# v of 14 heads turned by transposing transfers instead of TensorE transposes

## The chip, the cores and the metric

One core of a Trainium2 chip runs one launch of the kernel. The metric is the device time of that launch in microseconds, the median of several runs. The engines named below: PE is TensorE (matmuls, and PEld its weight loads), DVE is VectorE, ACT is ScalarE, POOL is GpSimd, SP is SyncE, which here only issues transfers.

## The reference, cut to what matters

One layer, 512 tokens (S) of width 2048 (D), 16 heads of 128: eight with stick-breaking attention (A), eight with banded chunk attention (B).

```python
h = rms_norm(x, norm_g[layer])
proj = jnp.einsum('bsd,de->bse', h, w_in[layer])
qa, ka, va, ga, qb, kb, vb, gb = jnp.split(proj, splits, axis=-1)
ya = stick_breaking_attention(split_heads(qa, N_HEADS_SB), ...)
yb = chunk_band_attention(split_heads(qb, N_HEADS_CH), ...)
mixed = jnp.concatenate([merge_heads(ya) * jax.nn.silu(ga),
                         merge_heads(yb) * jax.nn.silu(gb)], axis=-1)
x = x + jnp.einsum('bse,ed->bsd', mixed, w_out[layer])
```

In both kinds of attention the last step for a head is a product of weights (tokens by tokens) with v (tokens by 128). For that product v has to have its tokens on the partitions.

## The kernel before, in words

**Units and stages.** The input projection is computed transposed, with features on the partitions and tokens along the row. It is cut into 32 units of 256 columns. Four units make a group of two heads: unit 4g gives q, 4g+1 k, 4g+2 v and 4g+3 the gate; the head's number is n = 2g + h. Each product is done as a Winograd-like scheme with seven products instead of eight, and in two pieces of precision: every operand is split into a rounded high part and a low rest (ACT casts, DVE subtracts), and the matmuls of high by high, low by high and high by low are added up. 28 of the 32 units are "major" (`MAJOR`: units 3 to 30): such a unit runs seven stages, each of eight pairs of matmuls, one of 512 and one of 256 columns (lines 849 and 851). The weights of a stage are loaded by SP (line 520, and 536 for one block), summed by DVE (548) or by adding transfers from POOL (540, 559), and split by ACT (579) and DVE (580) into one of three buffers, which PE's stage releases when it is done.

**Joining a unit.** `chain(m)` brings a major unit's seven products together. Its working tile `c` has four spaces in the arena. It claims three of them when the unit's first product is there and the fourth after the second product; ACT copies products into `c` (607, 612, 615, 628), DVE adds and subtracts others (617 and the same helper line), and at the end one DVE sum of 1024 elements (632) adds the two halves of `c` and writes the unit's tile `t`, which is `C[g, kind]`, 128 features by two heads by 512 tokens. Then the four spaces are released and ("unit", u) is marked done.

**v of a head.** `v_turn` waits for the unit 4g+2, and for ("values", n-1), since there is one buffer for v. It takes one of three spare PSUM banks, issues four TensorE transposes of 128 by 128 (line 1529), and ACT copies the four blocks back into `C[g, 2]` while it scales each row by `rstd` (line 1534). Then ACT casts the high part of v (1537) and DVE writes the rest (1538) into the tile `v`. `values` multiplies the turned attention weights `wth` and `wtl` with it on PE. For the last heads the result is multiplied by the gate (1569) and stored by SP (1575). Attention weights are turned by PE too (1506); the first turn of head n waits for the values of head n-1.

**Order.** No engine chooses at run time. A list scheduler in the Python code plays the whole run through with its own cost per operation (`Op(engine, cost, fn, due, lag)`; `AC`, `DV` and `M` make such entries for ACT, DVE and PE) and writes each engine's instructions in the order in which it plays them, by due time. For a transfer it adds `lag` bytes at 290e3 bytes per microsecond and a landing of 2.4 us. On the chip each engine works through its list in order and waits at semaphores. SP's list is one queue for all loads and stores.

**The tail.** Units 28 to 31 are put in the order 28, 29, 27, 30, 31. After unit 31 the output projection runs over the stored heads; some of its operands (`xbwth`, `xbwtl`, written by ACT at line 763) lie in the buffers of the turned attention weights, and may be written only after the values of head 15.

Of the kernel before, what the change touches and what calls it, by code (L numbers as in the profile page):

```python
# [7 lines left out]

F32 = mybir.dt.float32
F32R = mybir.dt.float32r  # L10
BF16 = mybir.dt.bfloat16
AF = mybir.ActivationFunctionType
ALU = mybir.AluOpType
PSUM = bass.MemoryType.PSUM

P = 128
S = 512
D = 2048
NT = S // P
# [11 lines left out]
H = 256  # L31
# [46 lines left out]
def trunk_kernel(ctx: ExitStack, tc: tile.TileContext, xT, xn, wi, wqk, wo, ng, qg, kg, rel, out):  # L78
# [29 lines left out]
    act, dve, pe, sp, pool = nc.scalar, nc.vector, nc.tensor, nc.sync, nc.gpsimd  # L108

    def single(shape, name, dt=F32):  # L110
        return cp.tile(shape, dt, tag=name, name=name)

    def tmp(shape, tag, name, dt=F32, bufs=1):
        return wp.tile(shape, dt, tag=tag, name=name, bufs=bufs)
# [7 lines left out]
    rstd = single([P, NT], "rstd")  # L122
# [4 lines left out]
    R = single([P, S], "R")  # L127
# [17 lines left out]
    def avail(r):  # L145

        return all(r[1] <= x[0] or x[1] <= r[0] for x in taken.values())

    def claim(key, r):
        assert avail(r), (key, r, taken)  # L150
        taken[key] = r
        return arena[:, r[0]:r[1]] if r[0] < 100 * KB else parts[:, r[0] - 100 * KB:r[1] - 100 * KB]

    def unclaim(key):
        del taken[key]
# [7 lines left out]
    clock = [0.0]  # L163
# [5 lines left out]
    done = set()  # L169
# [19 lines left out]
    def DV(w, fn, due=None, n=1):  # L189
        return Op("DVE", (0.075 + 1.04e-3 * w) * n, fn, due)  # L190

    def AC(w, fn, due=None, n=1):
        return Op("ACT", (0.085 + 0.85e-3 * w) * n, fn, due)
# [4 lines left out]
    def M(cost, fn):  # L198
        return Op("PE", cost, fn, 0.0)
# [85 lines left out]
    def major(u):  # L285
        return u in MAJOR
# [87 lines left out]
    def need(k, before=0.0):  # L374

        return lambda: clock[0] + begins[k] - begins[position[0]] - before
# [119 lines left out]
    def stage(m, p):  # L496
        return step_of[MAJOR[m], p]
# [87 lines left out]
    def major_bank(u, p):  # L585
        return (3 * MAJOR.index(u) + 3 + BANK_OF[p]) % 5

    def chain(m):
        u = MAJOR[m]
        b = [banks[:, major_bank(u, p), :] for p in (0, 1, 5)]  # L590
        k = [at_step[stage(m, p)] for p in range(NP)]
        there = lambda p: lambda: ("stage", m, p) in done

        def free(p):
            x = major_bank(u, p)
            del holder[2 * x], holder[2 * x + 1]

        yield there(0)
        def space(i):
            w = (CMB[1] - CMB[0]) // 4  # L600
            return CMB[0] + i * w, CMB[0] + (i + 1) * w

        c = arena[:, CMB[0]:CMB[1]].rearrange("p (a b) -> p a b", a=4)
        for i in (0, 1, 2):
            yield lambda: avail(space(i))
            claim(("cmb", m, i), space(i))
        yield AC(512, lambda: act.copy(c[:, 0, :], b[0]), need(k[2], AHEAD[5]))
        done.add(("before", m, 2))
        yield there(1)
        yield lambda: avail(space(3))  # L610
        claim(("cmb", m, 3), space(3))
        yield AC(512, lambda: act.copy(c[:, 3, :], b[1]), need(k[3], AHEAD[5]))
        done.add(("before", m, 3))
        yield there(2)
        yield AC(512, lambda: act.copy(c[:, 2, :], b[0]), need(k[4], AHEAD[5]))
        done.add(("before", m, 4))
        join = lambda i, x, y, op=ALU.subtract: lambda: dve.tensor_tensor(out=c[:, i, :], in0=x, in1=y, op=op)  # L617
        yield there(3)
        yield DV(512, join(2, b[1], c[:, 2, :]), clock[0] + 3)
        free(1)  # L620
        yield there(4)
        yield DV(512, join(3, c[:, 3, :], b[0]), need(k[6], AHEAD[6]))
        done.add(("before", m, 6))
        yield there(5)
        yield DV(512, join(0, b[2], c[:, 0, :], ALU.add), clock[0] + 3)
        free(5)
        yield there(6)
        yield AC(512, lambda: act.copy(c[:, 1, :], b[0]), clock[0] + 1)
        free(0)
        _, t = yield from result(u, 0)  # L630
        t_ = t.rearrange("p a (b c) -> p (a b) c", c=H)
        yield DV(1024, lambda: dve.tensor_tensor(out=t_, in0=c[:, :, :H], in1=c[:, :, H:], op=ALU.add), clock[0] + 1.5)  # L632
        for i in range(4):
            unclaim(("cmb", m, i))
        done.add(("unit", u))
# [153 lines left out]
    def place(u, a, half):  # L789
        b = unit_banks(u, a)  # L790
        half = ALONE[u >= NU][half] if alone(u) else ENDS[half] if u == NU + 3 and a else half
        return b[half // 2] * 2 + half % 2
# [3 lines left out]
    for k in reversed(range(len(program))):  # L796
        n, x, a = program[k]
        u = steps_[n][0]
        b = major_bank(*steps_[n]) if major(u) else place(u, a, x[2]) // 2
# [121 lines left out]
    def result(u, a):  # L921

        if u >= NU:
            tag = (("wth", "wtl"), ("cv", "cg"))[u % 2][a]
            yield lambda: ("co", tag) not in done and all(("released", j, 1) in done for j in range(NJ) if HOME[j] == tag)
            done.add(("co", tag))
            t = tmp([P, 2, S], tag, f"co{u}_{a}")

            return [t.rearrange("p h (b f c) -> p h b f c", f=2, c=P)[:, :, :, f, :] for f in range(2)], t
        tag = ("cq", "ck", "cv", "cg")[u % 4]  # L930
        yield lambda: emptied(tag, u // 4 - 1)
        C[u // 4, u % 4] = t = tmp([P, 2, S], tag, f"c{u}")
        v = t.rearrange("p a (b c) -> p a b c", c=H)
        return [v[:, 0], v[:, 1]], t
# [257 lines left out]
    def emptied(tag, g):  # L1192

        n = head(g, 1)
        k = ("cq", "ck", "cv", "cg").index(tag)
        if g < 0:

            return ("released", k + 2, 0) in done
        if k == 0 and g % 2 and ("read", n, 2) not in done:
            return False  # L1200
        return (("read", n, 0), ("read", n, 1), ("c_v", g), ("store", g, 1))[k] in done
# [74 lines left out]
    C = {}  # L1276
    qk, vv, wt, wT, tm, bias = {}, {}, {}, {}, {}, {}
# [3 lines left out]
    def take(who):  # L1281

        yield lambda: len(owner) < len(SPARE)
        i = next(i for i in SPARE if i not in owner)
        owner[i] = who
        return i

    def give(i):
        del owner[i]
# [18 lines left out]
    def head(g, h):  # L1308
        return 2 * g + h
# [185 lines left out]
    def turn(n, b, src, k):  # L1495
# [20 lines left out]
        give(i)  # L1516
        done.add(("turned", n, b))

    def v_turn(g, h):
        n = head(g, h)  # L1520
        yield lambda: "R" in done and ("unit", 4 * g + 2) in done
        yield lambda: ("values", n - 1) in done if n else all(("staged", j, 0) in done for j in range(NJ))
        i = yield from take(("v", g, h))
        f = C[g, 2][:, h, :]
        b = banks[:, i, :]

        def fn():
            for t in range(NT):
                pe.transpose(b[:, t * P:(t + 1) * P], f[:, t * P:(t + 1) * P], ident)  # L1529

        yield M(0.5, fn)

        for t in range(NT):
            yield Op("ACT", 0.31, lambda: act.activation(f[:, t * P:(t + 1) * P], b[:, t * P:(t + 1) * P], AF.Copy, scale=rstd[:, t:t + 1]))
        give(i)
        d = vv[n] = tmp([P, 2, S], "v", "v", F32R)
        yield AC(512, lambda: act.copy(d[:, 0, :], f))
        yield DV(512, lambda: dve.tensor_tensor(out=d[:, 1, :], in0=f, in1=d[:, 0, :].bitcast(F32), op=ALU.subtract))
        done.add(("v read", n))
        done.add(("v", g, h))  # L1540
# [84 lines left out]
    for m in range(NM):  # L1625
        for x in ("A11", "A21", "A22", "A12"):
            spawn(block_load(m, x), (0, stage(m, 0)))
        spawn(block_s1(m), (0, stage(m, 0)))
        spawn(block_sums(m), (0, stage(m, 0)))
        for p in range(NP):  # L1630
            spawn(block_split(m, p), (0, stage(m, p)))
        spawn(chain(m), (0, 0))
# [3 lines left out]
    for g in range(NG):  # L1636
        for h in range(2):
            n = head(g, h)
            if g % 2:
                spawn(prep_q(g, h), (n, 0, 0))  # L1640
            for kind in range(2):
                spawn((prep_b if g % 2 else prep_a)(g, kind, h), (n, 0, kind))
            if g % 2:
                spawn(load_bias(g, h), (n, 0))
            spawn(score(g, h), (n, 1))
            spawn(v_turn(g, h), (n, 3))
            spawn(values(g, h), (n, 4))
        spawn(gates(g), (2 * g, 5))
# [42 lines left out]
```

## Time and profile before

| | |
|---|---|
| median of 3 runs | 904.73 us (904.24 to 905.43) |
| profiled execution | 904.54 us |
| its span | 902.8 us |
| TensorE transposes of v (line 1529) | 64, in 16 groups of four |
| their copies back (line 1534) | 64, 22.0 us of ACT |

The span is the time between the first and the last instruction that the profiler recorded; the device time has 1.7 us more around it. A group of instructions is shown with its line, engine, shapes and count, then busy time and mean duration in ns, then the idle time before it and what ended that. Matmuls are pipelined, so the durations of neighbours overlap: what one costs the stream is read from start to start.

### The profile page before, as it was taken

The page shows a single profiled execution, that of the slowest core. Times are in us where ns is not written, and L with a number is a line of the kernel's source. Part 1 is how long each engine was busy: PE and PEld are TensorE (multiplying, and loading weights), DVE is VectorE, ACT ScalarE, POOL GpSimd, SP SyncE. Part 2 cuts the span into 40 slices and gives each one's busy share as a digit, 9 for nine tenths or more (in the row PEclk, how much of TensorE's full clock was granted, in tenths as well). Part 3 has the DMA queues.
Part 4 walks back from the last instruction along what each step waited for, and adds up shares of the span by engine and source line. Part 5 has one row for each costly group of instructions (what it writes and reads, how often), then busy time and mean ns, then how long its engine had stood idle before and what let it go on. Part 6 is the DMA issues. An engine that isn't in the chain of part 4 may idle for free.

```text
span 902.8 us, 15448 instructions
## 1 busy us (share of the span) xinstructions
PE 896.8 (99%) x5504; PEld 801.3 (89%) x5504; DVE 767.1 (85%) x1251; ACT 637.5 (71%) x1203; POOL 69.9 (8%) x96
## 2 busy tenths in 40 slices
PE   9999999999999999999999999999999999999998
PEld 7898888888888888888888888888888988999997
DVE  7999989788898878788979787889878988988785
ACT  7876968797689658885876588868767885544342
POOL 0001000000000010000000000010000000101012
PEclk9999999999999999999999999999999999999999
DMA  9777787767676887587758765776664536656371
GB/s 310 250 211 169 156 182 183 178 153 184 160 177 142 199 193 171 139 176 198 167 136 215 184 167 136 188 191 158 152 168 126 185 115 208 158 196 181 125 187 47
DMA packets 187837, 156.22 MB, mean 173 GB/s; under 512 B 9072, under 2 KB 157552, under 8 KB 187760
## 3 DMA queue, kind: packets, MB, share of 16 engines
q1 hardware_dynamic: 177680, 122.58, 44.7%
q0 software_dynamic: 9792, 32.51, 22.3%
q8 instruction: 43, 0.70, 0.3%
q14 instruction: 34, 0.28, 0.1%
q10 hardware_dynamic: 288, 0.14, 0.1%
HBM read 117.45 MB, written 8.39 MB: 139 GB/s over the span
## 4 chain that ended last, share of the span: by engine, by line
PE 98%; ACT 1%; DVE 0%; issue 0%; DVEq 0%
PE banks L849 40%; PE banks L778 21%; PE banks L851 20%; PE banks L776 10%; PE banks L1506 2%; PE banks L839 2%; PE banks L1412 1%; PE banks L840 1%; PE banks L1529 1%; PE banks L1600 0%; ACT parts L579 0%; PE banks L1338 0%; DVE co L1054 0%; ACT W L1482 0%; PE banks L1339 0%
## 5 line engine op out<-in xcount | busy, mean ns | idle before, releaser
L849 PE MATMUL banks<-x,parts 128*128 128x512 f32 x1568 | 501.2, 401 | 0.0
L851 PEld LDWEIGHTS banks<-x,parts 128*128 128x128 f32 x1568 | 294.3, 188 | 70.0 <-DVE parts L580 0.7
L851 PE MATMUL banks<-x,parts 128*128 128x256 f32 x1568 | 309.8, 279 | 0.0
L580 DVE TENSOR_TENSOR parts<-arena,parts 128x1024 fp32r<-128x1024 f32 x196 | 239.0, 1221 | 67.1 <-ACT parts L579 66.7
L579 ACT CAST parts<-arena 128x1024 fp32r<-128x1024 f32 x196 | 205.9, 1051 | 111.2 <-PE banks L849 81.5
L849 PEld LDWEIGHTS banks<-x,parts 128*128 128x128 f32 x1568 | 240.5, 189 | 0.8
L778 PE MATMUL banks<-parts,x 128*128 128x256 f32 (+1 forms) x672 | 134.5, 298 | 0.0
L458 ACT CAST parts<-arena 128x1024 fp32r<-128x1024 f32 (+2 forms) x86 | 76.8, 908 | 68.0 <-PE banks L778 31.0
L778 PEld LDWEIGHTS banks<-parts,x 128*128 128x128 f32 x672 | 107.5, 191 | 3.7
L776 PE MATMUL banks<-parts,x 128*128 128x256 f32 (+1 forms) x336 | 100.3, 299 | 0.0
L462 DVE TENSOR_TENSOR parts<-arena,parts 128x1024 fp32r<-128x1024 f32 (+2 forms) x86 | 89.0, 1047 | 12.1 <-ACT parts L458 11.9
L778 PE MATMUL banks<-x,parts 128*128 128x256 f32 (+1 forms) x320 | 74.7, 326 | 0.0
L548 DVE TENSOR_TENSOR arena<-arena 128x1024 f32<-128x1024 f32 x56 | 68.3, 1219 | 4.8 <-DMA arena<-in_wi 4.4
L776 PEld LDWEIGHTS banks<-parts,x 128*128 128x128 f32 x336 | 63.9, 190 | 3.2
L778 PEld LDWEIGHTS banks<-x,parts 128*128 128x128 f32 x320 | 53.8, 190 | 5.4 <-DVE parts L462 0.5
L776 PE MATMUL banks<-x,parts 128*128 128x256 f32 (+1 forms) x160 | 52.9, 330 | 0.0
L540 POOL DMA_DIRECT2D arena<-arena x28 | 24.5, 873 | 340.8 <-DVE arena L617 97.3
L617 DVE TENSOR_TENSOR arena<-banks,arena 128x512 f32<-128x512 f32 x56 | 38.3, 683 | 5.9 <-PE banks L851 3.9
L559 POOL DMA_DIRECT2D arena<-arena x28 | 24.3, 869 | 215.8 <-DVE parts L580 152.3
L632 DVE TENSOR_TENSOR c<-arena 128x1024 f32<-128x1024 f32 x28 | 34.1, 1219 | 0.5
L1515 DVE TENSOR_TENSOR wtl<-banks,wth 128x128 fp32r<-128x128 f32 (+1 forms) x64 | 31.0, 484 | 3.6 <-ACT wth L1514 3.4
L776 PEld LDWEIGHTS banks<-x,parts 128*128 128x128 f32 x160 | 30.5, 191 | 3.1 <-ACT parts L458 0.3
(210 smaller groups left out, 1158.1 us busy)
## 6 DMA issues: line engine op xcount, KB each, us to landing
arena<-in_wi SPq DMA_DIRECT2D x308, 256.0 KB, 4.4
arena<-arena POOLq DMA_DIRECT2D x56, 512.0 KB, 5.5
arena<-in_wo SPq DMA_DIRECT2D x64, 256.0 KB, 3.1
xs<-in_xn SPq DMA_DIRECT2D x16, 256.0 KB, 4.0
mixd<-c SPq DMA_DIRECT2D x16, 256.0 KB, 4.0
out<-co SPq DMA_DIRECT2D x16, 256.0 KB, 4.2
x<-mixd SPq DMA_DIRECT2D x12, 256.0 KB, 4.0
co<-in_xn POOLq DMA_DIRECT2D x12, 256.0 KB, 6.1
```

The costliest lines, as they stand in the source:

```text
L458: act.copy(whl[n, part][:, 0, c], t)
L462: yield DV(c.stop - c.start, lambda: dve.tensor_tensor(out=l[:, c], in0=t, in1=h[:, c].bitcast(F32), op=ALU.subtract), need(k, 0.5))
L548: add = lambda x, due: DV(1024, lambda: dve.tensor_tensor(out=r("A21"), in0=r("A21"), in1=r(x), op=ALU.add), due)
L579: yield AC(1024, lambda: act.copy(v[:, 0, :], t), need(k, AHEAD[3]))
L580: yield DV(1024, lambda: dve.tensor_tensor(out=v[:, 1, :], in0=t, in1=v[:, 0, :].bitcast(F32), op=ALU.subtract), need(k, AHEAD[4]))
L617: join = lambda i, x, y, op=ALU.subtract: lambda: dve.tensor_tensor(out=c[:, i, :], in0=x, in1=y, op=op)
L632: yield DV(1024, lambda: dve.tensor_tensor(out=t_, in0=c[:, :, :H], in1=c[:, :, H:], op=ALU.add), clock[0] + 1.5)
L776: pe.matmul(o, lh, rh, start=start, stop=False, **kw)
L778: pe.matmul(o, x, y, start=False, stop=stop and (x is ll) != early, **kw)
L849: pe.matmul(both, mats[n][:, 0, j, :], X[j][:, :, i, :], start=p in (0, 1, 5) and j == 0, stop=False, skip_group_check=True)
L851: pe.matmul(o[:, :H], mats[n][:, 1, j, :], X[j][:, 0, i, :], start=False, stop=j == NJ - 1, skip_group_check=True)
L1515: yield DV(w, lambda: dve.tensor_tensor(out=tl[:, blocks, :], in0=tv, in1=th[:, blocks, :].bitcast(F32), op=ALU.subtract))
```

## The change

For the units 4g+2 that are major (seven of them, groups 1 to 7) `chain` ends differently. DVE adds the halves of `c` in place, one head at a time, and ACT writes each head's 512 words to `t` as two planes of 16-bit halves: all low halves, then all high halves. `v_turn` of such a head calls `v_by_dma`: SP issues one transposing transfer of the 128 by 1024 16-bit values into the buffer of `v`, as eight blocks of 128 columns; ACT joins the two planes to 32-bit words again in `C[g, 2]`; four ACT operations scale them in place by `rstd`; and the split into high part and rest is as before. No PSUM bank and no matmul are used. The two heads of group 0 keep the TensorE transposes. `chain` also claims each of its four spaces when it is first needed, in every major unit, and releases them in two halves in the changed units.

```diff
@@ chain
-        for i in (0, 1, 2):
+        def own_space(i):
             yield lambda: avail(space(i))
             claim(("cmb", m, i), space(i))
+
+        yield from own_space(0)
         yield AC(512, lambda: act.copy(c[:, 0, :], b[0]), need(k[2], AHEAD[5]))
...
-        yield lambda: avail(space(3))
-        claim(("cmb", m, 3), space(3))
+        yield from own_space(3)
...
+        yield from own_space(2)
...
+        yield from own_space(1)
         yield AC(512, lambda: act.copy(c[:, 1, :], b[0]), clock[0] + 1)
         free(0)
         _, t = yield from result(u, 0)
+        if u % 4 == 2:
+
+            for h in range(2):
+                x = c[:, 2 * h:2 * h + 2, :]
+                yield DV(512, lambda: dve.tensor_tensor(out=x[:, :, :H], in0=x[:, :, :H], in1=x[:, :, H:], op=ALU.add), clock[0] + 1.5)
+                yield AC(1024, lambda: act.copy(t[:, h, :].bitcast(U16).rearrange("p (a b n) -> p b n a", a=2, b=2),
+                                                x[:, :, :H].bitcast(U16).rearrange("p b (n a) -> p b n a", a=2)), clock[0] + 1.5)
+                for i in (2 * h, 2 * h + 1):
+                    unclaim(("cmb", m, i))
+            done.add(("unit", u))
+            return
@@ new functions, and v_turn
+    def by_dma(planes, turned):
+
+        w = planes.shape[-1]
+        return Op("SP", 1.5, lambda: sp.dma_start(turned.rearrange("p (a b) -> p a b", b=P), planes, transpose=True), None, lag=P * 3 * w)
+
+    def v_by_dma(g, h):
+        n = head(g, h)
+        yield lambda: "R" in done and ("unit", 4 * g + 2) in done
+        yield lambda: ("values", n - 1) in done
+        f = C[g, 2][:, h, :]
+        t_ = tmp([P, 4 * S], "v", "vt", U16)[:, :2 * S]
+        yield by_dma(f.bitcast(U16), t_)
+        yield AC(1024, lambda: act.copy(f.bitcast(U16).rearrange("p (n a) -> p a n", a=2), t_.rearrange("p (a n) -> p a n", a=2)))
+        for t in range(NT):
+            yield Op("ACT", 0.22, lambda: act.activation(f[:, t * P:(t + 1) * P], f[:, t * P:(t + 1) * P], AF.Copy, scale=rstd[:, t:t + 1]))
+        d = vv[n] = tmp([P, 2, S], "v", "v", F32R)
+        yield AC(512, lambda: act.copy(d[:, 0, :], f))
+        yield DV(512, lambda: dve.tensor_tensor(out=d[:, 1, :], in0=f, in1=d[:, 0, :].bitcast(F32), op=ALU.subtract))
+        done.add(("v read", n))
+        done.add(("v", g, h))
+
     def v_turn(g, h):
         n = head(g, h)
+        if major(4 * g + 2):
+            yield from v_by_dma(g, h)
+            return
```

More of the change, by code (lines that the diff above doesn't have):

```diff
@@ L10 @@
 F32R = mybir.dt.float32r
-BF16 = mybir.dt.bfloat16
+U16 = mybir.dt.uint16
 AF = mybir.ActivationFunctionType
```

## The prediction

> **What bounds the kernel now.** I read the page first (busy times, the chain that ended last), then the table of stretches, to see whether any stretch has another limit, then TensorE's order of time around one of the removed groups.
>
> ```profile
> PE 896.8 (99%) x5504; PEld 801.3 (89%) x5504; DVE 767.1 (85%) x1251; ACT 637.5 (71%) x1203; POOL 69.9 (8%) x96
> ...
> PE 98%; ACT 1%; DVE 0%; issue 0%; DVEq 0%
> ```
>
> The chain of waits is 98% TensorE. A busy PE could still hide waiting, so the stretches of 20 us follow; columns are length, then busy time and count of PE, PEld, DVE, ACT, POOL, then granted clock, DMA share, GB/s.
>
> ```profile
> 180.00:200.00 20.00, 20.00 (x121) 17.66 (x120) 16.74 (x35) 18.58 (x38) 1.06 (x3) 1.00 0.67 162
> ...
> 300.00:320.00 20.00, 20.00 (x120) 17.61 (x119) 15.28 (x25) 10.81 (x21) 1.89 (x3) 1.00 0.94 230
> ...
> 700.00:720.00 20.00, 20.00 (x151) 19.00 (x150) 19.04 (x38) 17.56 (x43) 0.14 (x1) 1.00 0.53 176
> 720.00:740.00 20.00, 20.00 (x130) 17.91 (x129) 17.48 (x45) 17.23 (x37) 0.73 (x1) 1.00 0.31 106
> ...
> sum 900.00, PE 896.80 PEld 801.33 DVE 767.13 ACT 637.46 POOL 69.93; mean PE 19.93 PEld 17.81 DVE 17.05 ACT 14.17 POOL 1.55
> ```
>
> PE is at 20.00 of 20 in the fullest ACT stretch (18.58) and in the fullest of the tail: it waits for nobody, at the granted clock of 1.00. So a microsecond of matmul time taken from the middle is a microsecond of the end, as long as ACT and DVE keep handing over operands.
>
> **The change part by part: the PE time removed.** Columns: start, duration, engine, line.
>
> ```profile
> 164.28 0.63 PE L849 MATMUL banks<-x,parts 128*128 128x512 f32 x2
> 164.74 0.40 PE L851 MATMUL banks<-x,parts 128*128 128x256 f32 x2
> 164.98 0.60 PE L1529 MATMUL banks<-ident,c 128*128 128x128 f32 x4
> 165.33 0.71 PE L849 MATMUL banks<-x,parts 128*128 128x512 f32 x2
> 165.88 0.40 PE L851 MATMUL banks<-x,parts 128*128 128x256 f32 x2
> ```
>
> Durations overlap, so I count starts. The four transposes hold the stream for 165.33 - 164.98 = 0.35 us. The pair behind them is slow too: from its L849 to its L851 it takes 0.55 where the pair ahead took 0.46, another 0.09. One head costs 0.44, and 14 heads cost 14 x 0.44 = 6.2 us. Fourteen, because group 0's unit is not major. Bounds: 14 x 0.35 = 4.9 if the slow start stays, 6.2 otherwise; more than that isn't there to be removed.
>
> **ACT and DVE.**
>
> ```profile
> L579 ACT CAST parts<-arena 128x1024 fp32r<-128x1024 f32 x196 | 205.9, 1051 | 111.2 <-PE banks L849 81.5 <-issue 12.6 <-DVE arena L548 5.2
> L1534 ACT ACTIVATE c<-banks,rstd 128x128 f32<-128x128 f32 x64 | 22.0, 370 | 0.9 <-PE banks L1529 0.9
> L1491 ACT ACTIVATE W<-W,st 128x128 f32<-128x128 f32 x8 | 3.2, 396 | 0.2
> L632 DVE TENSOR_TENSOR c<-arena 128x1024 f32<-128x1024 f32 x28 | 34.1, 1219 | 0.5
> L617 DVE TENSOR_TENSOR arena<-banks,arena 128x512 f32<-128x512 f32 x56 | 38.3, 683 | 5.9 <-PE banks L851 3.9
> ```
>
> No row has a 16-bit copy. The nearest is the 1024-wide CAST, 1.05 us, which I take; below, half of it, 0.53, if pairs of halves went at once; above, twice it, 2.1, if the two-step order of the 16-bit halves costs. Seven units make two such copies each, 14 heads one each: 28 x 1.05 = 29 us of ACT (15 to 59). The four scalings per head now read SBUF instead of a bank: L1491's 0.396 against L1534's 0.370, 14 x 4 x 0.026 = 1.5 us. ACT goes from 637.5 to about 668 us, 74%. DVE's 1024-wide sum becomes two 512-wide ones: 7 x (2 x 0.683 - 1.219) = 1.0 us. These 32 us lie beside PE. Their cover is how far the splits run ahead:
>
> ```profile
> ACT parts L579 <- PE banks L849: 81.5, 81, 3.7
> ...
> DVE arena L548 <- DMA arena<-in_wi: 4.4, 5, 1.6
> ```
>
> ACT's split waited 81 times, 81.5 us in all (longest 3.7), for PE to give a buffer back: ACT is ahead of PE, held by three split buffers. A stage of PE is four pairs of 0.70 (164.28 to 165.33 less the transposes is 0.70 for two), that is 2.8 us; I take one stage, 2.8 us, as what ACT may lose at once. Singles of 1.05 fit. Were that cover gone, the added ACT would land on PE whole.
>
> The splitting of the unit's last step keeps the four combining spaces longer: about 0.68 + 1.05 for the first half, then the same for the second, instead of 1.22. The next unit wants its first space back after its stage 0 and before its stage 2, between 2.8 and 5.6 us on. The first half fits (about 2.9 with the copy ahead of it); the second is wanted 2.8 us later. Cost nothing, at most 1 us x 7 if a queue of two sits between.
>
> **The transfer, SP and the later v.** The transposing transfer has no row. The code's planner counts 1.5 us of SP, 1.36 of transfer and 2.4 of landing, 5.3 us. Nearest rows, both plain and of 256 KB, issue to landing minimum/median/maximum, of the store of a head (L1575) and of the weight loads (L520):
>
> ```profile
> DMA to landing us min/median/max: 2.0/4.0/6.2
> ```
> ```profile
> DMA to landing us min/median/max: 2.9/4.3/7.9
> ```
>
> I take 5 us, near the medians and with some room for the turning; the ends are 2.0, and 8 x 2.0 = 16 if the eight 128-column blocks went one after another at the shortest landing. SP is in order: each transfer waits there for ACT's copy and for the matmuls of the head before, with weight loads behind it. Loads were late only 4.4 us in five waits (the row of L548 above), so SP held for 1.5 us costs nothing; held past the loads' lead it would show as more of that row.
>
> Each v is ready about 3 us (longer unit) + 5 - 0.6 (transfer for transposes) + 1.05 = 8 us later. Odd heads have the room. Of the even ones the last, head 14, has the least:
>
> ```profile
> 705.88 0.59 ACT L628 COPY arena<-banks 128x512 f32<-128x512 f32 x1
> ...
> 708.74 0.60 PE L1529 MATMUL banks<-ident,c 128*128 128x128 f32 x4
> ...
> 712.57 0.69 DVE L1538 TENSOR_TENSOR v<-c,v 128x512 fp32r<-128x512 f32 x1 [0.44 <-ACT v L1537]
> ...
> 716.04 0.50 PE L776 MATMUL banks<-wth,v 128*128 128x512 f32 x1
> ...
> 727.97 0.33 PE L1506 MATMUL banks<-ident,W 128*128 128x128 f32 x1
> ...
> 743.62 0.39 PE L776 MATMUL banks<-wth,v 128*128 128x512 f32 x1
> ...
> 745.71 0.40 ACT L763 CAST xbwth<-xm 128x256 fp32r<-128x256 f32 x1
> ...
> 748.94 0.39 PE L776 MATMUL banks<-parts,xbwth 128*128 128x512 f32 x1
> ```
>
> Head 14's v, now ready at 713.3, would be ready at about 721, and its values matmuls start 5 us later; PE takes projection products in the meantime. Head 15's first turn, 727.97, needs those values done (about 723): still met. Head 15's v then comes at about 735 to 737, before its matmuls at 743.62. This margin matters, because 5.3 us behind head 15's values (748.94) PE starts on blocks that may only be written after them. But between 700 and 740 ACT has 5.2 us idle, and two unit copies plus two head copies bring 4.2. I charge 1.2 us of PE waiting for this tail (0 to 4.2).
>
> **The sum.** Against the profiled execution's 904.54 us (its span 902.8; the median of the three is 904.73, 0.2 above): 904.54 - 6.2 + 1.2 = 899.5 us. With each term at its end, 898.3 to about 903.
>
> [...] Row first: a plain 256 KB transfer lands in 4.0 us, and no row here turns anything. [...]
>
> **The rivals.**
> (a) The transfer is slow and holds ACT: slower than before. ACT is in order and its re-joining copy stands where the planner expects the data, 5.3 us after the issue. A transfer of T us holds ACT, and the weight splits behind it, for T - 5.3; past the cover of 2.8 us PE stops. Price: 14 x (T - 8.1). It eats the 6.2 us saved from T = 8.5 on. At T = 9.5: 14 x 1.4 = 20 us, 918 us; at 16: 111 us, 1009 us. For it: eight blocks, 2-byte pieces, a DMA share up to 0.94. Against: the longest plain transfer of L520 was 7.9 us. [...] Chance 0.19.
> (b) ACT becomes the limit where it is fullest: no change. 180 to 200 us has 1.4 us of ACT idle, the tail 5.2; seven units with 1.05 x 4 us each would lose some 0.5 to 1 us apiece, and the tail up to 4.2. 904.54 - 6.2 + 7 x 0.6 + 2 = 904.5 us. For it: the tail's margins; against: 10.81 us in the stretch from 300, and buffers that let ACT run ahead. Chance 0.17.
> (c) The change doesn't do what it says, if the matmuls left behind don't close up because DVE sets their pace: then 904.5 + 1. DVE's 19.04 in 700 to 720 speaks for it, PE's 20.00 everywhere against. Chance 0.03.
>
> **How the numbers follow.** Forecast 0.61 (899.5, own range 898.0 to 902.7). The measurement tells about 0.2%, 1.8 us, from no change. Faster: the forecast, 0.61, plus the good edge of (b), 0.02: 0.63. Same: most of (b) and (c), 0.15. Slower: (a) and the bad edge of (b), 0.22. The range begins at 898.0 (whole saving, nothing lost, and 0.3 us of spread between runs) and must reach through (b) and the first part of (a), T up to about 9: 904.54 - 6.2 + 14 x 0.9 = 911.
>
> **What would show it.** Right: L1529 is down to 8 matmuls, PE's busy time falls by about 6 us and the stretches stay at 20.00; SP's transposing transfers land in 4 to 7 us; the re-joining copies wait little. Wrong: ACT's copy heads the list of waits on a DMA, with PE waiting for splits (L580) right behind each of 14 places: rival (a). PE idle near 745 to 760 waiting for the blocks written after head 15: the tail margin was mis-sized. ACT near 20 in the stretches where units end, with PE below 20: rival (b).

## The result and the profile after

The changed kernel takes **957.75 us** (median of 4 runs, 957.18 to 959.28) against 904.50 us of the kernel before on the same chip: a ratio of 1.0589, 95% interval 1.0571 to 1.0608. It is 5.9% slower; 899.5 us was forecast.

The page of the profile of after, first the busy times, then the granted clock in 40 slices of the span, the shares of the chain that ended last, and one of its groups:

```profile
span 957.5 us, 15389 instructions
...
PE 910.3 (95%) x5448; PEld 808.8 (84%) x5448; DVE 769.3 (80%) x1258; ACT 716.9 (75%) x1231; POOL 70.0 (7%) x96
...
PEclk9999999999989998999899989999999999999999
...
PE 81%; ACT 9%; issue 4%; DVE 4%; DMA 0%; SPq 0%; ACTq 0%; DVEq 0%
...
L639 ACT COPY c<-arena 128x1024 uint16<-128x1024 uint16 x14 | 67.4, 4817 | 0.0
```

PE no longer fills the span: it is idle for 957.5 - 910.3 = 47.2 us, where it was for 902.8 - 896.8 = 6.0. ACT has entered the chain with 9%, and the reason stands in the last line: the copy that writes a head's two planes takes 4.82 us, 14 times, 67.4 us in all, where the prediction had 1.05 us each. ACT's busy time rose by 79.4 us (637.5 to 716.9) instead of by 30.

A second thing is odd: PE has 56 matmuls fewer and is *busier* by 13.5 us. The view of cores says why: its clock was not granted in full throughout.

```profile
core 0: 957.5 us, clock 0.978
```

The mean of 0.978 over 957.5 us is what 2 x 0.022 x 957.5 = 42 us at half clock give, an estimate; added up over stretches of 2 us, of which the lowest are at 0.50, it is 41 us. Before, the mean was 1.00.

The transfer, on which the prediction laid most weight, did better than forecast. The view of its line (duration at SP minimum/median/maximum, first and last start; then issue to landing), and that of the copy which joins the planes again:

```profile
L1536 SPq DMA_TRANSPOSE vt<-c x14: 1246/1278/2896, 169.2 to 780.5; - x14
...
DMA to landing us min/median/max: 3.1/3.1/5.6
```
```profile
L1545 ACT COPY c<-vt x14: 1336/1360/1381, 181.2 to 784.5; 128x1024 uint16<-128x1024 uint16 x14
...
  DMA vt<-c: 1.2, 2
```

It lands in 3.1 us (5 forecast), and ACT waited for it twice, 1.2 us in all. What PE waited for stands in the list of waits (total us, times, longest):

```profile
DVE parts L580 <- ACT parts L579: 85.7, 75, 4.7
...
PE banks L863 <- ACT arena L609: 19.1, 6, 4.0
...
PE banks L863 <- ACT arena L613: 10.0, 4, 3.5
...
PE banks L1520 <- ACT W L1505: 6.0, 2, 5.9
...
PE banks L1352 <- DVE qk L1468: 4.0, 2, 2.0
```

L609 and L613 are ACT's copies of finished products out of the PSUM banks (607 and 612 before), L863 the 512-column matmul that needs the bank. So PE waited 29.1 us for ACT to empty banks, in 10 places. The last two lines, 10.0 us more, are of the same kind: the longest wait for L1505 (5.85 us, ended at 763.65) is for an ACT operation that stands behind a plane copy, and at 362.94 DVE's L1468 had itself waited 3.39 us for an ACT operation behind another. Splits of weights, DVE's L580, are not what PE waited for: they come to 0.2 us, on its weight loads. One of the 10 places, in the order of time:

```profile
261.42 4.87 ACT L639 COPY c<-arena 128x1024 uint16<-128x1024 uint16 x1
...
267.03 0.58 ACT L609 COPY arena<-banks 128x512 f32<-128x512 f32 x1
...
267.66 0.73 PE L863 MATMUL banks<-x,parts 128*128 128x512 f32 x2 [2.54 <-ACT arena L609]
...
268.04 4.79 ACT L639 COPY c<-arena 128x1024 uint16<-128x1024 uint16 x1
...
273.56 0.59 ACT L613 COPY arena<-banks 128x512 f32<-128x512 f32 x1
273.71 1.23 DVE L580 TENSOR_TENSOR parts<-arena,parts 128x1024 fp32r<-128x1024 f32 x1 [4.64 <-ACT parts L579]
...
274.20 1.22 PE L863 MATMUL banks<-x,parts 128*128 128x512 f32 x2 [3.49 <-ACT arena L613]
```

ACT takes the first plane copy at 261.42 and the second at 268.04. Behind the first the bank copy comes at 267.03 and PE has stood 2.54 us; behind the second it comes at 273.56 and PE has stood 3.49 us; DVE waits 4.64 us for ACT's split. Two holds of 4.8 us come within 12 us, at the end of the unit. The table of stretches of 2 us (columns as in the prediction's) shows what follows:

```profile
270.00:272.00 2.00, 0.71 (x5) 0.42 (x3) 0.00 (x0) 2.00 (x1) 0.00 (x0) 1.00 1.08 275
272.00:274.00 2.00, 0.00 (x0) 0.00 (x0) 0.29 (x1) 2.00 (x3) 0.00 (x0) 0.83 0.62 98
274.00:276.00 2.00, 1.80 (x5) 1.59 (x6) 0.93 (x1) 2.00 (x5) 0.00 (x0) 0.50 0.03 8
...
278.00:280.00 2.00, 2.00 (x8) 1.71 (x7) 1.06 (x2) 0.55 (x3) 0.00 (x0) 0.50 0.79 225
...
284.00:286.00 2.00, 2.00 (x14) 1.73 (x12) 2.00 (x3) 1.97 (x5) 0.00 (x0) 1.00 1.04 235
```

After the gap the granted clock falls to 0.50 and stays there until about 280: eight matmuls in 2 us instead of 14. Each of the seven units has such a place.

### The profile page after: what moved, and what is told of

It is laid out like the page before. It is cut to its first block, busy times and chain, and to the rows that moved or that the text cites. A ratio compares the mean times of both kernels' runs of the same rounds, so it can differ in the third digit from the quotient of the medians.

```text
span 957.5 us, 15389 instructions
## 1 busy us (share of the span) xinstructions
PE 910.3 (95%) x5448; PEld 808.8 (84%) x5448; DVE 769.3 (80%) x1258; ACT 716.9 (75%) x1231; POOL 70.0 (7%) x96
## 4 chain that ended last, share of the span: by engine, by line
PE 81%; ACT 9%; issue 4%; DVE 4%; DMA 0%; SPq 0%; ACTq 0%; DVEq 0%
PE banks L863 33%; PE banks L792 18%; PE banks L865 16%; PE banks L790 9%; ACT c L639 3%; PE banks L1520 2%; PE banks L853 2%; DVE parts L580 2%; ACT parts L579 1%; PE banks L1426 1%; PE banks L854 1%; ACT W L1503 1%; ACT arena L631 0%; PE banks L1638 0%; ACT parts L458 0%
## 5 line engine op out<-in xcount | busy, mean ns | idle before, releaser
L863 PE MATMUL banks<-x,parts 128*128 128x512 f32 x1568 | 509.9, 407 | 29.1 <-ACT arena L609 19.1
L865 PEld LDWEIGHTS banks<-x,parts 128*128 128x128 f32 x1568 | 299.2, 191 | 71.7 <-DVE parts L580 0.2
L865 PE MATMUL banks<-x,parts 128*128 128x256 f32 x1568 | 313.1, 281 | 0.0
L580 DVE TENSOR_TENSOR parts<-arena,parts 128x1024 fp32r<-128x1024 f32 x196 | 238.8, 1220 | 86.6 <-ACT parts L579 85.7
L863 PEld LDWEIGHTS banks<-x,parts 128*128 128x128 f32 x1568 | 244.7, 192 | 31.4 <-ACT arena L609 20.2
L792 PE MATMUL banks<-parts,x 128*128 128x256 f32 (+1 forms) x672 | 134.6, 298 | 0.0
L792 PEld LDWEIGHTS banks<-parts,x 128*128 128x128 f32 x672 | 107.6, 191 | 3.7
L462 DVE TENSOR_TENSOR parts<-arena,parts 128x1024 fp32r<-128x1024 f32 (+2 forms) x86 | 89.2, 1047 | 18.9 <-ACT parts L458 18.7
L790 PE MATMUL banks<-parts,x 128*128 128x256 f32 (+1 forms) x336 | 100.5, 299 | 0.0
L548 DVE TENSOR_TENSOR arena<-arena 128x1024 f32<-128x1024 f32 x56 | 68.2, 1218 | 13.6 <-DMA arena<-in_wi 13.2
L792 PE MATMUL banks<-x,parts 128*128 128x256 f32 (+1 forms) x320 | 76.0, 330 | 0.0
L639 ACT COPY c<-arena 128x1024 uint16<-128x1024 uint16 x14 | 67.4, 4817 | 0.0
L790 PEld LDWEIGHTS banks<-parts,x 128*128 128x128 f32 x336 | 64.0, 190 | 3.5 <-DVE co L1035 0.2
L792 PEld LDWEIGHTS banks<-x,parts 128*128 128x128 f32 x320 | 55.2, 195 | 5.2 <-DVE parts L462 0.2
L790 PE MATMUL banks<-x,parts 128*128 128x256 f32 (+1 forms) x160 | 53.7, 336 | 0.0
L1520 PE MATMUL banks<-ident,W 128*128 128x128 f32 x160 | 29.7, 286 | 6.3 <-ACT W L1505 6.0
```

What stands on the lines that cost most here:

```text
L462: yield DV(c.stop - c.start, lambda: dve.tensor_tensor(out=l[:, c], in0=t, in1=h[:, c].bitcast(F32), op=ALU.subtract), need(k, 0.5))
L548: add = lambda x, due: DV(1024, lambda: dve.tensor_tensor(out=r("A21"), in0=r("A21"), in1=r(x), op=ALU.add), due)
L580: yield DV(1024, lambda: dve.tensor_tensor(out=v[:, 1, :], in0=t, in1=v[:, 0, :].bitcast(F32), op=ALU.subtract), need(k, AHEAD[4]))
L639: yield AC(1024, lambda: act.copy(t[:, h, :].bitcast(U16).rearrange("p (a b n) -> p b n a", a=2, b=2), x[:, :, :H].bitcast(U16).rearrange( ...
L790: pe.matmul(o, lh, rh, start=start, stop=False, **kw)
L792: pe.matmul(o, x, y, start=False, stop=stop and (x is ll) != early, **kw)
```

## The experiments

**The theory**: the slow copy alone does it, because in its order each written 16-bit half lies in the other plane from the one before. ACT is held, banks and splits come late, PE stands, its clock drops. **Rivals**: the earlier claim and split release of the spaces; a plan that counts the copy at 0.955 us and so puts it at a bad place; the transfer. Times are medians; "before" ran beside them on the same chip.

### The same copy in the order of the planes

```diff
-                yield AC(1024, lambda: act.copy(t[:, h, :].bitcast(U16).rearrange("p (a b n) -> p b n a", a=2, b=2),
-                                                x[:, :, :H].bitcast(U16).rearrange("p b (n a) -> p b n a", a=2)), clock[0] + 1.5)
+                yield AC(1024, lambda: act.copy(t[:, h, :].bitcast(U16).rearrange("p (a b n) -> p a b n", a=2, b=2),
+                                                x[:, :, :H].bitcast(U16).rearrange("p b (n a) -> p a b n", a=2)), clock[0] + 1.5)
```

Same values to the same places, but all low halves are written first, then all high halves. Every engine's instructions stand in the same order as in after.

> One edit: ACT writes the two 16-bit planes one after the other (innermost index the word) instead of alternating between them for every word; cost told to the planner, and so every engine's order, unchanged. Theory H (the 14 alternating copies of 4.8 us hold ACT, and all of the loss follows from that): the copies fall to 1.1 to 1.4 us, as the joining copy's 1.36, TensorE idle falls from 47 us to 6 to 9, the granted clock is 1.00 again, and the time is 898.5 to 902. Rival T (the rest of the change, that is 31 us more of ACT, the later v, SP held by the transfers, the claims of space, costs a good part): the copies are short and the time still stays above 908. Rival W (any strided 16-bit copy is slow): the copies stay above 3 us and the time above 940.

Measured: **903.18 us**, before 904.62, ratio 0.9982 (0.9973 to 0.9991), a little above the 898.5 to 902 that the theory expected. The page, and the line's view:

```profile
PE 893.1 (99%) x5448; PEld 796.0 (88%) x5448; DVE 767.3 (85%) x1258; ACT 667.1 (74%) x1231; POOL 70.4 (8%) x96
...
PE 91%; DVE 4%; ACT 3%; issue 1%; DMA 0%; SPq 0%; DVEq 0%; ACTq 0%
```
```profile
L639 ACT COPY c<-arena x14: 1032/1045/1051, 164.5 to 707.3; 128x1024 uint16<-128x1024 uint16 x14
```

One reordering takes 54.6 us off: the copy takes 1.045 us, the mean clock is 1.000. With instructions and order the same, the difference of the spans, 957.5 - 901.4 = 56.1 us, is PE's idle time, 47.2 - 8.3 = 38.9, and slower matmuls, 910.3 - 893.1 = 17.2. The waits listed above account for all of the idle time: those for banks (29.1) and for L1468 (4.0) are gone, and that for L1505 falls from 6.0 to 0.2. The theory holds for the whole loss. The transfer and the joining copy are still in, so they aren't its cause. But 903.18 lies some 3.7 us above the forecast, which had the copy at the same 1.05; three experiments further down go after that.

### The claims of the spaces alone

```diff
-        if u % 4 == 2:
+        if False:
...
-        if major(4 * g + 2):
+        if False:
```

> Only the later claims of the four combining spaces; v is turned by TensorE and the unit joined by one sum, as before. H: nothing of the loss sits here, 903 to 906. T, if the claims cost: above 908.

Measured: 904.84 us, before 904.62, ratio 1.0003 (0.9994 to 1.0012). The later claims cost nothing, as the prediction had it. The split release isn't in this kernel.

### A plan that knows the slow copy

```diff
-                yield AC(1024, lambda: act.copy(...
+                yield Op("ACT", 4.4, lambda: act.copy(...
```

> The alternating copies stay, but the planner is told 4.4 us for each instead of 0.96, so that it can put casts and bank copies ahead of them. H as a matter of the hold's length: a copy of 4.8 us still stands in front of the copies of banks that TensorE needs within a stage of 2.8 us, so it stays slow, 935 to 960. H as a matter of the planner's error only: ACT has room (75% busy), and the time falls below 915.

Measured: 952.23 us, ratio 1.0524 (1.0507 to 1.0540). The loss is 47.6 us instead of after's 53.2, so a plan that knows the copy's length gets back 5.6 of it.

### The copies by themselves

A small program, run once, makes each copy six times, 128 by 1024, and nothing of the layer is computed. It is not quite free of neighbours: the DVE copies (L51, L53) ran beside ACT's L35, L47 and the first L37; ACT's other copies ran alone.

> Not the layer: only copies of 128x1024 elements on an otherwise idle core, six of each order, 16-bit on ACT: contiguous; alternating between two planes on the write; plane after plane; writing every other halfword (the joining copy); reading alternately from two planes; alternating with planes of 16 elements; the alternating and the plane order with 32-bit elements; and the first two orders on DVE. H: alternating 16-bit writes 4.3 to 4.8 us, plane after plane and the joining order 1.0 to 1.4. If the slowness is in far jumps, planes of 16 elements are fast and 32-bit is slow too; if it is in partial writes of a word with another address in between, 32-bit is fast. W: all strided orders are slow.

The groups of its page (busy us, mean ns of one):

```profile
L37 ACT COPY b<-src 128x1024 uint16<-128x1024 uint16 x6 | 28.5, 4744 | 0.0
L45 ACT COPY b<-src 128x1024 uint16<-128x1024 uint16 x6 | 28.4, 4727 | 0.2
L51 DVE COPY d<-src 128x1024 uint16<-128x1024 uint16 x6 | 16.6, 2775 | 0.2
L47 ACT COPY dst<-src 128x1024 f32<-128x1024 f32 x6 | 12.2, 2030 | 0.0
L49 ACT COPY dst<-src 128x1024 f32<-128x1024 f32 x6 | 8.5, 1414 | 0.0
L41 ACT COPY b<-src 128x1024 uint16<-128x1024 uint16 x6 | 8.0, 1328 | 0.2
L43 ACT COPY b<-src 128x1024 uint16<-128x1024 uint16 x6 | 6.9, 1157 | 0.2
L35 ACT COPY b<-src 128x1024 uint16<-128x1024 uint16 x6 | 6.4, 1069 | 0.0
L39 ACT COPY b<-src 128x1024 uint16<-128x1024 uint16 x6 | 6.3, 1050 | 0.2
L53 DVE COPY d<-src 128x1024 uint16<-128x1024 uint16 x6 | 4.2, 694 | 0.2
```

L35 is contiguous. L37 writes as after does, alternating between two planes: 4744 ns, close to after's 4817, and the five that ran without a neighbour took 4.73 us each. L39 writes plane by plane, 1050. L41 is the joining copy (every other half written), 1328. L43 *reads* alternating, 1157. L45 alternates between planes of 16 elements instead of 512, 4727. L47 and L49 are alternating and plane order with 32-bit words, 2030 and 1414. L51 and L53 are L37 and L39 on DVE, 2775 and 694. L47 and L51 were taken beside each other, so part of their length may be the neighbour's; L37, L45 and L39 are free of this. So what costs in these rows is writing that alternates between two planes at every element (1050 to 4744 ns; writing every other half, 1328, costs far less); reading so costs a tenth more (1157), the distance between the planes, 32 or 1024 bytes, nothing (4727 against 4744), and with 16-bit elements it is dear (4.5 times) where with 32-bit words it is 1.4 times at most (2030 against 1414). Per element that is 3.6 ns more than plane order with 16 bits ((4744 - 1050) / 1024) and 0.6 ns or less with 32. No run here had planes closer than the 32 bytes of L45, and none shows what in the write takes the time.

### The last group left on TensorE

In addition to the order of the planes, group 7 keeps its transposes.

```diff
-        if u % 4 == 2:
+        if u % 4 == 2 and u < NU - 4:
...
-        if major(4 * g + 2):
+        if major(4 * g + 2) and g < NG - 1:
```

> Plane order as in e1, but the last group (heads 14 and 15) keeps the TensorE transposes: 12 heads by transfer. Theory L (of the 4 to 5 us that e1 gives back, 1.5 to 2 sit in the tail, where head 15's values come no earlier while TensorE arrives earlier): one head pair less saves 0.9 less and the tail's wait of about 1.7 goes: 901.5 to 902.7, below e1. Rival B (what is given back is spread over all units, a matter of ACT's 31 us more): 903.3 to 904, above e1, since only two heads' saving is lost.

Measured: **901.92 us**, before 904.82, ratio 0.9969 (0.9958 to 0.9981), the lowest of all, and within the 901.5 to 902.7 that theory L expected. In the table of stretches, the reordered kernel first, then this one (before has 20.00 of PE in the first, second and fourth of these stretches and 19.73 from 680 to 700):

```profile
360.00:380.00 20.00, 19.67 (x116) 17.30 (x117) 16.05 (x30) 18.41 (x37) 1.02 (x2) 1.00 0.77 178
540.00:560.00 20.00, 19.70 (x117) 17.24 (x116) 15.06 (x26) 18.44 (x36) 1.01 (x2) 1.00 0.79 166
680.00:700.00 20.00, 19.55 (x114) 16.90 (x114) 16.62 (x40) 18.25 (x41) 0.86 (x1) 1.00 0.40 111
740.00:760.00 20.00, 18.66 (x85) 15.20 (x85) 17.28 (x29) 11.54 (x21) 0.00 (x0) 1.00 0.61 206
```
```profile
740.00:760.00 20.00, 20.00 (x94) 16.76 (x93) 17.41 (x31) 11.73 (x20) 0.00 (x0) 1.00 0.66 200
```

In the reordered kernel PE stands 1.34 us in the stretch from 740; here it doesn't. That is the tail of the prediction, at the place that it named:

```profile
745.41 0.41 ACT L777 CAST xbwth<-xm 128x256 fp32r<-128x256 f32 x1 [1.39 <-PE banks L792]
...
745.87 0.50 PE L790 MATMUL banks<-parts,xbwth 128*128 128x512 f32 x1 [0.49 <-ACT xbwth L777]
...
746.98 0.41 DVE L778 TENSOR_TENSOR xbwth<-xm,xbwth 128x256 fp32r<-128x256 f32 x1
...
747.44 0.50 PE L792 MATMUL banks<-parts,xbwth 128*128 128x512 f32 x1 [0.84 <-DVE xbwth L778]
```

(From the reordered kernel, in order of time.) The blocks that may be written only after head 15's values are late for PE by 0.49 and 0.84 us.

### The planner's costs set to what was measured

The reordered kernel, with the joining copy told as 1.27, a scaling as 0.31, SP as 1.3, and a third of the transfer's lag; alone, and then with the last group left on TensorE.

```diff
-        return Op("SP", 1.5, ..., lag=P * 3 * w)
+        return Op("SP", 1.3, ..., lag=P * w)
...
-        yield AC(1024, lambda: act.copy(...
+        yield Op("ACT", 1.27, lambda: act.copy(...
-            yield Op("ACT", 0.22, lambda: act.activation(...
+            yield Op("ACT", 0.31, lambda: act.activation(...
```

> As e1 with all 14 heads; the planner is told what the trace shows: joining copy 1.27, scaling 0.31 each, 1.3 us of SP and a shorter transfer. L: the order of the tail is a little better, 902 to 903.2. Rival: the planner's costs are not what gives the microseconds back, 903 to 904.

> e4 and e5 together. L: 900.5 to 902.5, the best of the four. Rival B: 903 to 904.

Measured: 909.45 us (ratio 1.0058, 1.0045 to 1.0070) and 903.45 us (0.9990, 0.9982 to 0.9999). Both are worse than the same kernel with the old costs, by 6.3 and 1.5 us, and both miss what was expected of them. The first shows it most in the tail:

```profile
740.00:760.00 20.00, 16.99 (x70) 13.17 (x70) 17.46 (x29) 11.80 (x23) 0.00 (x0) 0.91 0.52 165
```

PE stands 3 us there and the clock drops to a mean of 0.91. Costs closer to the measured ones gave another order, and that order happened to be worse; why it falls so was not followed further.

### The copy in four pieces

After's alternating copy, cut into four of 256 elements each, told at 1.15 us. Theory H1 says that the length of one hold matters, H2 that the total at that place does.

```diff
-                yield AC(1024, lambda: act.copy(...
+                tp = t[:, h, :].bitcast(U16).rearrange("p (a b n) -> p b n a", a=2, b=2)
+                xp = x[:, :, :H].bitcast(U16).rearrange("p b (n a) -> p b n a", a=2)
+                for b_ in range(2):
+                    for n_ in (0, P):
+                        yield Op("ACT", 1.15, lambda: act.copy(tp[:, b_, n_:n_ + P, :], xp[:, b_, n_:n_ + P, :]), clock[0] + 1.5)
```

> The alternating write order of the change, but each copy cut into four of 256 elements (about 1.2 us each), and the planner told 1.15 for each: ACT's total is as long as with the change (about 717 us), no hold is longer than 1.2 us. Theory H1 (the loss comes from the length of one hold against a lead of about 1 us that the copies of banks have): TensorE's idle falls from 47 to below 15 us, the granted clock stays at 1.00, the time is 903 to 912. Rival H2 (the loss comes from ACT's total time around the units' ends): still above 930.

Measured: 968.14 us, ratio 1.0704 (1.0687 to 1.0720), slower than after.

```profile
L643 ACT COPY c<-arena 128x256 uint16<-128x256 uint16 x56 | 75.4, 1348 | 0.1
```
```profile
268.00:270.00 2.00, 0.29 (x3) 0.14 (x2) 1.97 (x4) 2.00 (x4) 0.09 (x1) 1.00 0.75 145
272.00:274.00 2.00, 1.17 (x3) 0.98 (x4) 0.00 (x0) 2.00 (x4) 0.00 (x0) 0.50 0.82 242
```

The same places get 75.4 us in pieces of 1.35. At the place shown in the second fence (columns as before: PE first, ACT fourth) the eight pieces start between 265.25 and 278.31, with one or more other ACT operations between any two, and ACT is busy without a break from 264 to 282. Still PE stands (964.7 - 916.8 = 47.9 us of idle time, where H1 expected under 15): the first bank copy, L609, comes at 272.21, behind four pieces. So H1 falls: no single hold is long, and the loss is there. The order in which the plan put the pieces and the bank copy has its part, which this run does not separate from their total.

### The holds put into the kernel before

Here the kernel before, transposes and all, gets two alternating copies per unit 4g+2, in six groups, into a tile that nobody reads, after the spaces have been released: no transfer and no split release. The unit counts as done only after its copies, so its v is turned later too (group 1's first transposes start at 178.3 us with two copies told, at 165.0 before); no wait of PE for v is in the list of that run. Told at 4.4 us, then at 0.955; then only one copy per unit; then the same two as eight pieces, due 2 us apart.

```diff
...
+        if u % 4 == 2 and u < NU - 4:
+            yield lambda: emptied("cg", u // 4 - 1)
+            s_ = tmp([P, 2, S], "cg", f"s{u}")
+            for h in range(2):
+                yield Op("ACT", 4.4, lambda: act.copy(s_[:, h, :].bitcast(U16).rearrange("p (a n) -> p n a", a=2),
+                                                       t[:, h, :].bitcast(U16).rearrange("p (n a) -> p n a", a=2)), clock[0] + 1.5)
```

The second has `0.955` in place of `4.4`, the third `range(1)`. The fourth hands the tile to a generator of its own, so that the unit is done at once, and the unit behind waits for the pieces before its last sum:

```diff
+            for n_ in range(0, 512, P):
+                yield Op("ACT", 1.25, lambda: act.copy(sp_[:, n_:n_ + P, :], tp_[:, n_:n_ + P, :]), d0 + 2 + 2 * (4 * h + n_ // P))
...
+        if u % 4 == 3 and 6 < u < NU - 1:
+            yield lambda: ("pieces", u - 1) in done
...
+            spawn(pieces(u, s_, t), (0, 0))
```

> The kernel before, with its TensorE transposes, its single sum and its release of the four spaces untouched; behind the release, in six units (groups 1 to 6), ACT makes two alternating 16-bit copies of 4.8 us each from the unit's tile into a tile that is free then. Their result is read by nobody. The planner is told 4.4 us each. Theory S (TensorE waits because the slow copies keep the combining spaces that the next unit's bank copies need): with the spaces free and the planner able to put the bank copies and casts between, the loss is small, 904 to 915. Theory A (58 us more of ACT, close behind a unit's end, is the loss itself): six sevenths of the 56 us, 940 to 955.

> As e8, but the planner is told 0.955 us for each copy, as in the change. S: the bank copies are no longer behind a space, but still behind the hold in ACT's queue where the planner put them so; somewhat slower than e8, 910 to 930. A: like e8, 940 to 955.

> e8 with one alternating copy of 4.8 us per unit instead of two (six holds in all). If a hold costs the same each time, half of e8's loss: 928. If there is a cover of 2.8 us per unit, as the prediction had it, (4.8 - 2.8) x 6 = 12 us: 917. If what ACT has done ahead carries one hold whole: 904 to 908.

> The kernel before with as much added ACT work as e8 or a little more (six units, eight alternating pieces of 256 elements each, about 1.3 us apiece, read by nobody), but due one every 2 us over the 16 us after the unit's end, beside the unit instead of ahead of what follows it; the planner is told 1.25. Theory P (it is the burst behind a unit's end that ACT can't take; spread out it has room, since ACT is busy 71%): 904 to 915. Theory A (each added microsecond of ACT costs about one wherever it stands): 940 to 955.

| copies per unit | time, us | ratio (interval) | lost per unit, us |
|---|---|---|---|
| two, told | 952.16 | 1.0521 (1.0490 to 1.0551) | 47.3 / 6 = 7.9 |
| two, untold | 945.74 | 1.0450 (1.0404 to 1.0496) | 40.9 / 6 = 6.8 |
| one, told | 921.70 | 1.0177 (1.0083 to 1.0271) | 16.0 / 6 = 2.7 |
| eight pieces, spread | 929.05 | 1.0258 (1.0198 to 1.0318) | 23.4 / 6 = 3.9 |

Before beside them was 904.87 for the first two and 905.69 for the others. Each row is two runs, and the intervals of the last two are wide: one copy may cost 1.3 to 4.1 us per unit. Against the reordered kernel after loses 54.6 / 7 = 7.8 us per unit, and the kernel whose plan knew the copy (952.23 - 903.18) / 7 = 7.0. The two copies without the transfer and the split release give 6.8 where the plan did not know them and 7.9 where it did: about the same. That takes out the rival of the spaces, for the claims and for the release. The planner's knowledge isn't the cause either: telling it made this kernel slower (945.74 to 952.16), where it made after faster. The pages of two told, one, and the spread pieces:

```profile
PE 911.9 (96%) x5504; PEld 808.7 (85%) x5504; DVE 766.8 (81%) x1251; ACT 690.5 (73%) x1212; POOL 69.9 (7%) x96
```
```profile
PE 899.4 (98%) x5504; PEld 802.9 (87%) x5504; DVE 766.8 (84%) x1251; ACT 663.2 (72%) x1207; POOL 70.1 (8%) x96
...
L639 ACT COPY s<-c 128x1024 uint16<-128x1024 uint16 x6 | 28.9, 4824 | 0.0
```
```profile
PE 904.8 (98%) x5504; PEld 802.2 (87%) x5504; DVE 766.1 (83%) x1251; ACT 685.3 (74%) x1247; POOL 70.1 (8%) x96
...
L594 ACT COPY s<-c 128x256 uint16<-128x256 uint16 x48 | 66.4, 1386 | 0.9 <-DMA mixd<-c 0.9
```

With one hold PE's idle time is 918.1 - 899.4 = 18.7 us, 12.7 more than before's 6.0: 2.1 us per hold of 4.8. By that ACT could lose 2.7 us there unseen, close to the 2.8 that the prediction read from one stage (2.1, if the whole 2.7 us lost per hold is counted, slower matmuls included; anything from 0.7 to 3.5 by the interval). The second hold finds the cover spent and costs 7.9 - 2.7 = 5.2 us (some 3 to 7 by the intervals, so that it costs more than its own length is not shown). Of the 33.0 us by which the span with two exceeds the span with one, 20.5 are PE's idle time and 12.5 slower matmuls, at a mean clock of 0.989 against 0.997. Spread over 16 us, even more work (66.4 us in pieces) costs half, between the two times expected. So the burst counts, but not alone: 11 us of ACT per unit don't fit without loss even when spread. How the loss divides between the two the runs leave open.

## Why the prediction was wrong, point by point

1. **What bounds the kernel: right.** PE set the end, and each us that it stands or slows is a us of the end: in after 38.9 of standing and 17.2 of slowness make up the 56.1 us.
2. **The step that failed: the price of the 16-bit copies** ("The nearest is the 1024-wide CAST, 1.05 us, which I take; ... above, twice it, 2.1, if the two-step order of the 16-bit halves costs"). The copy that joins measured 1.36, between these ends; the one that writes the planes measured 4.82, more than twice the upper end. The prediction looked at the number of elements and the width, took both copies for one operation with one answer, and didn't ask which index runs innermost on the written side. The doubt was named, but its price was doubled by guess, with no row; up to 2.1 us a copy still fits under the cover of 2.8, so the copies stood in the sum at nothing, and no case of the range had them.
3. **The cover: near in size, by luck in part, and wrongly used.** 2.8 us was taken per single copy; one hold showed 2.1 to 2.7. But it was read from the lead of the weight splits, and what PE waited for in after were copies out of banks, whose lead the prediction did not look at. And two copies come at the end of one unit, within 12 us. At 1.05 each they fit; at 4.82 they don't. "Were that cover gone, the added ACT would land on PE whole" then came true by the number: 14 x (4.82 - 1.05) = 53 us more of ACT, and 54.6 us more of time. That the numbers meet is luck: PE stood only 38.9 us longer, and slower matmuls, which the prediction did not have, made up the rest.
4. **Rival (a): half of the mechanism was right, its cause wrong.** ACT was held and PE stood behind it, but at the unit's end and not behind the joining copy, and for banks to be emptied, not for splits. The transfer that was to hold it landed in 3.1 us, median and minimum, against 5 forecast and 8.5 at which it would have eaten the saving. That is below the plain store of the same size before (4.0 us median), from which, with the loads (4.3), the 5 was estimated; the longest, 5.6 us, is far from the upper end of 16 us for eight blocks one after another.
5. **The spaces: right; SP and ACT's total: only in part.** Claims cost nothing. Issuing the transfer held SP 1.28 us (1.5 forecast), but the sign that the prediction named, DVE waiting at L548 for weight loads, did grow, from 4.4 us in five waits to 12.8 us in seven, the longest 4.5, in the reordered kernel. Ahead of the two longest of these waits (ended at 378.20 and 558.48) SP had waited 7.3 and 7.8 us for a split of DVE, not for a transposing transfer; the cause was not followed further. They did not reach PE, whose list there too has 0.2 us for splits. With the plane copies at their forecast price, ACT's total was 667.1 us, 668 in the prediction. That is luck in part: the joining copies cost 14 x 0.31 = 4.3 us more than forecast, and what made up for it was not followed.
6. **The saving: over-counted, which the big miss hides.** In the reordered kernel the plane copies are at their forecast price, and still the span fell only from 902.8 to 901.4, not by 5.0. PE's busy time fell by 3.7 us instead of 6.2. Counted from start to start as in the prediction, all v transposes hold PE's stream for 5.69 us before and 0.71 with the eight that are left, so 5.0 us went, as 14 x 0.35 = 4.9 had it. The other 1.3, for the slow pairs behind, was never there to be had: from start to start the pairs (L849 and L851 before) sum to the same, within 0.1 us, in both kernels. A further 1.3 came back on L790 and L792, which make the products with v and of the output projection; why was not followed. Idle time rose by 2.3 us: 1.34 in the tail, where 1.2 was charged, and 0.8 in the three other stretches shown, for which nothing was charged. Those last waits had no term in the sum. The sum's worse end was also added wrongly: 904.54 - 4.9 + 4.2 is 903.8, not about 903.
7. **The clock of 1.00** was read off the rows of before and kept for the kernel after. A gap of PE was priced at its length; here 38.9 us of gaps brought 17.2 us of slow matmuls with them.

## What to carry to other kernels

Price a copy by the order in which it writes, not by its element count (4.82 against 1.05 us here for the same 1024): look which index is innermost on the output side, and loop over the contiguous one there; this one reordering turned 5.9% slower into 0.2% faster. Where a row for such a form is missing, a program of ten copies gives it before the kernel is built around it. An engine that is busy 71% on average may still have no room for a burst: compare the burst with the lead of the buffers at that place (here about 2 to 3 us by the medians), and where a gap at TensorE is possible, count the slower matmuls behind it too (here 17.2 us behind 38.9 us of gaps).

## What the hardware showed that was not expected

- Copies that alternate between two places in what they write: 4744 ns against 1050 for 1024 16-bit elements on ACT, 2775 against 694 on DVE, 2030 against 1414 with 32-bit words on ACT (2775 and 2030 taken beside each other); reading so costs only 1157. Why 16-bit elements pay so much more than 32-bit ones the runs don't show.
- The granted clock went to 0.50 after gaps of PE of 2.5 and 3.5 us and stayed there for some 6 us, at full load; over the run the mean was 0.978, by estimate about 42 us at half clock.
- The transposing transfer of 256 KB within SBUF lands sooner (3.1 us) than the plain store of the same size to DRAM did in the kernel before (4.0 us).
